# One activation buffer's low half, 64 bytes further on, in the token mixers as well

## The chip, the core and the metric

One Trainium2 chip; the kernel runs on one of its cores. The metric is the device time of one execution in microseconds, and of several executions the median. The profile is one execution of the same program recorded by the hardware profiler; its times count from the first instruction.

## What is computed

A decoder layer on 512 tokens of width 1024, in float32: a SwiGLU feed-forward network (width 2816), then a token mixer, then a second feed-forward network, each between a norm before and a norm after it.

```python
for l in range(DEPTH):
    x = x + 0.5 * rms_norm(swiglu_ffn(rms_norm(x, norm_pre[l, 0]), ffn1_w_in[l], ffn1_w_out[l]), norm_post[l, 0])
    mixed = token_mixer(rms_norm(x, norm_pre[l, 1]), w_mix_in[l], ...)
    x = x + rms_norm(mixed, norm_post[l, 1])
    x = x + 0.5 * rms_norm(swiglu_ffn(rms_norm(x, norm_pre[l, 2]), ffn2_w_in[l], ffn2_w_out[l]), norm_post[l, 2])
```

The mixer projects the normed x with one matrix (`h @ w_in`, 3592 columns), runs two recurrences over chunks of tokens (HGRN2 and mLSTM heads) and projects their outputs with `w_out`.

## The kernel before

**Two parts instead of one float32.** Every large product is made of three matmuls in the form float32r: each operand is split into a high part (a rounded copy, ScalarE) and a low part (what the rounding lost, VectorE), and high x high, high x low and low x high are summed in PSUM. So each buffer of activations or weights holds a high half of 1024 words per partition and a low half of 1024 words.

**Where the activations lie.** The transposed activations lie in four buffers `xq0` to `xq3`, made in `Layer.__init__` (L101 to L106). Each is one quarter: 256 tokens by half of the 1024 features. `xq0` has the first 256 tokens and features 0 to 511, `xq1` the same tokens and features 512 to 1023, `xq2` and `xq3` the other tokens. `xq0` alone is 32 words longer than the others (`2 * STEP`, `STEP` = 16 words = 64 bytes). There are two views of it. `self.xh[0]` is the view of the feed-forward networks: its low half begins 16 words later than the end of its high half. `self.xq[0]` is the view of the mixers: its low half follows at once, as in the other quarters. `xh` is used by `part` (L334, which writes it) and by `open_ffn` (L538, which makes the networks' operands of it); `xq` is used by `to_t` (L328, which writes it) and by `xop` (L153), through which every matmul of the mixers reads it.

**Where the weights lie.** One buffer `w` has four slots of 2048 words. `lie` (L207) puts a slot's contents at a displacement out of `LIES` (L64): 0, -16, -80 or 48 words, in another order for the mixers' wide weights ("mix": -16 first) than for the networks' first layers ("any": 0 first).

**What the mixers do with the quarters**, in order of time:

- `head4` (L508): four products `head_mm` (L498, its matmuls are L503), each 24 matmuls for the first 256 tokens: eight high x high, eight that read the activations' low half, eight that read the weights' low half. The weights are stationary, 256 columns of activations stream by.
- `forget_gates` (L1106): the same four products for the other 256 tokens, by `in_mm` and `in_k` (L489; matmuls L493): 24 matmuls each, of `xq2` and `xq3` alone.
- `job_f` (L937): eight products over all tokens, also by `in_k` (L493): for each of eight feature blocks six matmuls, and in the first four blocks one of the six reads the low half of `xq0`.
- `job_rows` (L1284, matmuls L1291): 32 matmuls for the gates' rows, four of them on the low half of `xq0`.
- `job_t` (L953), `mix_out0` and `mix_out1`: here the activations are stationary (128 x 128) and 512 columns of weights stream by, three matmuls at a time in `mm3` (L146; L148 high x high, L149 high x low, L150 low x high). L150 loads the activations' low half.

Between these stand small float32 matmuls and transposes of the recurrences. Which weights are loaded, split and freed when is planned by `weights` and `feed` ahead of use; the mixers fill the recurrences' waits with `job_*` work by `fill`.

The feed-forward networks' first layers are 7 products for each pair of column blocks (`prod`, matmuls L559). The product "p1" reads `xq0`: 24 matmuls in a row, of which the second eight read its low half, 64 bytes further on already. The second layers are L816 and L824.

Of the kernel before, what the change touches and what calls it, by code (L numbers as in the profile page):

```python
# [16 lines left out]
D = 1024  # L17
# [5 lines left out]
RAW, WBUF, PAD, LATE, NEXT, FRONT, STEP = 3, 4, 128, 112, 64, 96, 16  # L23
PAIRS = NF // 2
HALF = T // 2
KH = ND // 2
# [40 lines left out]
class Load:  # L67


    def __init__(self, key, src, a, b, ring="raw", depth=3, ahead=3, group=None):  # L70
        self.key, self.src, self.a, self.b, self.ring, self.depth, self.ahead = key, src, a, b, ring, depth, ahead
        self.group = group
# [12 lines left out]
class Layer:  # L85
    def __init__(self, ctx, tc, aps):
        self.tc, self.nc = tc, tc.nc
        self.__dict__.update(aps)
        nc = self.nc
        pool = lambda name, **kw: ctx.enter_context(tc.tile_pool(name=name, bufs=1, **kw))  # L90
        self.cp, self.wp, self.sp, self.psp = pool("cp"), pool("wp"), pool("sp"), pool("psp", space=PSUM)
        self.uid, self.hold = 0, ()
        self.wt, self.free, self.slot = None, deque(), {}

        self.ident = self.cp.tile([P, P], F32, name="ident")
        make_identity(nc, self.ident)
        self.nhalf = self.cp.tile([P, 8], F32, name="nhalf")
        nc.gpsimd.memset(self.nhalf, -0.5)
        self.xs = self.cp.tile([P, NT, D], F32, name="xs")

        xq = {n: self.cp.tile([P, 2 * D + 2 * STEP * (n == 0)], F32R, name=f"xq{n}") for n in (1, 2, 3, 0)}  # L101
        self.xt = [xq[n] for n in range(4)]
        self.xq = [t[:, : 2 * D].rearrange("p (b k t) -> p b k t", b=2, k=KH) for t in self.xt]

        x0 = self.xt[0].rearrange("p (b x) -> p b x", b=2)[:, :, :D].rearrange("p b (k t) -> p b k t", k=KH)
        self.xh = [x0, *self.xq[1:]]  # L106
        self.prm = self.cp.tile([P, 36], F32, name="prm")

    def nm(self, s):
# [42 lines left out]
    def xop(self, k, part, t0, t1):  # L152
        q = self.xq[2 * (t0 // HALF) + k // KH]  # L153
        return q[:, part, k % KH, t0 % HALF : (t1 - 1) % HALF + 1]
# [175 lines left out]
    def part(self, i, h, src):  # L330

        pv = self.turn(src, h)
        v = slice(i * P, (i + 1) * P)
        dst = self.xh[h][:, :, :, v]  # L334
        yield
        self.nc.scalar.copy(dst[:, 0], pv)
        yield
        self.nc.vector.tensor_tensor(dst[:, 1], pv, dst[:, 0].bitcast(F32), op=ALU.subtract)
        yield
        self.nc.scalar.copy(self.xf[h][:, :, v], pv)  # L340
        yield
# [189 lines left out]
    def open_ffn(self, ctx):  # L531

        hp = self.hpool = ctx.enter_context(self.tc.tile_pool(name=self.nm("hp"), bufs=1))
        self.hf = hp.tile([P, NF, T], F32, name=self.nm("hf"))
        self.xf = [self.hf[:, j : j + 2, :].rearrange("p a (b t) -> p (a b) t", t=HALF) for j in (NF - 4, NF - 2)]
        sq = [hp.tile([P, 2 * D + PAD], F32R, tag="s", bufs=3, name=self.nm("sq")) for _ in range(3)]
        self.sq = [self.both(self.place(t, LATE)) for t in sq]
        xq = [self.both(x) for x in self.xh]  # L538
        self.stay = [self.place(t, NEXT) for t in sq]
        self.left = {"p1": xq[0], "p2": xq[1], "p4": xq[3], "p5": xq[2], "p6": self.sq[2], "p7": self.sq[1], "p3": self.sq[0]}  # L540
        self.left.update({"c1": xq[0], "c2": xq[1], "c3": xq[0], "c4": xq[1]})
        self.left.update({"e1": xq[2], "e2": xq[3], "e3": xq[2], "e4": xq[3]})
        self.gs, self.held, self.copies = [], {}, []
        self.hs, self.bank, self.later, self.u, self.q, self.had = deque(), {}, deque(), {}, {}, set()
# [1171 lines left out]
```

## Time and profile before

| | us |
|---|---|
| median of 3 runs | 948.15 |
| the runs | 946.64, 948.79, 948.15 |
| the profiled execution, its time | 947.97 |
| the profiled execution, first to last instruction | 946.2 |
| TensorE (PE) busy | 937.4 |
| VectorE (DVE) busy | 776.1 |
| ScalarE (ACT) busy | 489.4 |
| GpSimd (POOL) busy | 121.2 |
| first matmul of the mixers (L503) to the last (L150) | 344.3 to 609.5 |

PE is the engine of the matmuls, PEld its weight loads, which run beside the matmuls. A group of instructions is shown as `line engine operation tile<-tiles`, its count, busy time and mean duration in ns. A matmul's recorded duration (276 ns and the like) is longer than the distance from one matmul to the next, since matmuls are pipelined: the distance is read from the chain of waits, where a row is the start in us, the length in us, and how many instructions of one line follow each other without a gap (16.32 us for 144 matmuls are 113.3 ns from one to the next).

### The profile page before, as it was taken

Reading aid. Unit: us, or ns where it says so; the run is one execution under the profiler, and the core shown is the slowest. Engines: PE = TensorE matmul, PEld = TensorE weight load, DVE = VectorE, ACT = ScalarE, POOL = GpSimd, SP = SyncE. Lnnn points to the kernel's source line nnn. Section 1 sums busy time; section 2 is a strip of 40 time slices with the busy share of each in tenths; the row PEclk is TensorE's granted clock in tenths of the full one; section 3 lists DMA queues with packets and bytes.
Section 4 is the critical chain, followed back from the end, with each engine's and each line's share of the span. In section 5 each row is a group of like instructions: output and inputs, shape, how many; then the busy total and the mean of one; then the engine's idle time right before and its main releaser. Section 6 shows DMA issues by size and latency. Waiting matters only on the chain.

```text
span 946.2 us, 18146 instructions
## 1 busy us (share of the span) xinstructions
PE 937.4 (99%) x7531; PEld 903.5 (95%) x7531; DVE 776.1 (82%) x1052; ACT 489.4 (52%) x691; POOL 121.2 (13%) x176
## 2 busy tenths in 40 slices
PE   9999999999999999999999999999999999999997
PEld 7999999999999999998887888899999999999997
DVE  6899999999789786698846665798998899988984
ACT  7645444555446457956632444664444444654541
POOL 3530000000001045200001310353000000000102
PEclk9999999999999999999999999999999999999999
DMA  9244343244232034321312124324333333124212
GB/s 319 84 134 134 106 141 111 91 131 119 97 108 85 23 92 126 98 67 46 89 45 68 45 89 139 107 68 135 112 112 118 107 112 112 67 90 135 70 44 89
DMA packets 81677, 96.13 MB, mean 102 GB/s; under 512 B 4117, under 2 KB 61497, under 8 KB 81594
## 3 DMA queue, kind: packets, MB, share of 16 engines
q1 hardware_dynamic: 81306, 94.44, 31.6%
q8 instruction: 59, 0.97, 0.4%
q10 hardware_dynamic: 288, 0.52, 0.2%
q14 instruction: 24, 0.20, 0.1%
HBM read 92.85 MB, written 2.10 MB: 100 GB/s over the span
## 4 chain that ended last, share of the span: by engine, by line
PE 62%; ACT 1%; DVE 0%; issue 0%; POOL 0%; DVEq 0%; POOLq 0%; ACTq 0%
PE ps L559 23%; PE ps L816 8%; PE ps L493 6%; PE ps L148 5%; PE ps L150 5%; PE ps L149 5%; PE ps L824 4%; PE ps L1206 2%; PE ps L316 1%; PE ps L503 1%; PE ps L1380 0%; PE ps L1291 0%; PE ps L1487 0%; PE ps L1460 0%; PE ps L1246 0%; PE ps L1484 0%
## 5 line engine op out<-in xcount | busy, mean ns | idle before, releaser
L242 ACT CAST w<-raw 128x1024 fp32r<-128x1024 f32 (+1 forms) x228 | 235.5, 1039 | 252.5 <-PE ps L559 89.7
L244 DVE TENSOR_TENSOR w<-raw,w 128x1024 fp32r<-128x1024 f32 (+1 forms) x228 | 283.2, 1248 | 42.6 <-ACT w L242 42.4
L559 PE MATMUL ps<-xq,w 128*128 128x256 f32 x2016 | 237.9, 277 | 0.0
L559 PEld LDWEIGHTS ps<-xq,w 128*128 128x128 f32 x2016 | 233.4, 188 | 0.0
L559 PE MATMUL ps<-sq,w 128*128 128x256 f32 x1440 | 169.8, 276 | 0.0
L559 PEld LDWEIGHTS ps<-sq,w 128*128 128x128 f32 x1440 | 166.2, 188 | 0.0
L816 PE MATMUL ps<-w,hs 128*128 128x256 f32 x1344 | 158.1, 276 | 0.3
L816 PEld LDWEIGHTS ps<-w,hs 128*128 128x128 f32 x1344 | 154.8, 188 | 0.7 <-DVE hs L752 0.7
L258 DVE TENSOR_TENSOR raw<-raw,raw 128x1024 f32<-128x1024 f32 x64 | 80.1, 1251 | 0.7
L148 PE MATMUL ps<-w,xq 128*128 128x512 f32 x192 | 78.9, 411 | 0.1
L150 PE MATMUL ps<-w,xq 128*128 128x512 f32 x192 | 74.9, 392 | 0.0
L149 PE MATMUL ps<-w,xq 128*128 128x512 f32 x192 | 74.9, 391 | 0.0
L404 POOL TENSOR_SCALAR col<-col 128x1 f32<-128x1 f32 x24 | 10.5, 438 | 494.4 <-ACT junk L403 494.3
L493 PE MATMUL ps<-xq,w 128*128 128x256 f32 x480 | 58.0, 282 | 0.0
L493 PEld LDWEIGHTS ps<-xq,w 128*128 128x128 f32 x480 | 56.8, 189 | 0.5 <-issue 0.5
L258 POOL TENSOR_TENSOR raw<-raw,raw 128x1024 f32<-128x1024 f32 x16 | 43.1, 2697 | 51.6 <-DVE w L244 42.3
L148 PEld LDWEIGHTS ps<-w,xq 128*128 128x128 f32 x192 | 36.1, 188 | 8.3 <-issue 0.9
L150 PEld LDWEIGHTS ps<-w,xq 128*128 128x128 f32 x192 | 36.0, 188 | 8.2 <-DVE xq L323 0.3
L149 PEld LDWEIGHTS ps<-w,xq 128*128 128x128 f32 x192 | 36.2, 188 | 6.7 <-issue 0.2
L751 ACT CAST hs<-hf 128x1024 fp32r<-128x1024 f32 x28 | 29.4, 1051 | 22.2 <-PE ps L824 22.2
L824 PE MATMUL ps<-w,hs 128*128 128x256 f32 x336 | 40.4, 276 | 0.0
L824 PEld LDWEIGHTS ps<-w,hs 128*128 128x128 f32 x336 | 39.1, 188 | 0.0
(250 smaller groups left out, 1143.1 us busy)
## 6 DMA issues: line engine op xcount, KB each, us to landing
raw<-in_ffn_w_in_dram SPq DMA_DIRECT2D x88, 512.0 KB, 3.8
raw<-in_ffn_w_out_dram SPq DMA_DIRECT2D x44, 512.0 KB, 3.7
raw<-in_w_mix_in_dram SPq DMA_DIRECT2D x28, 512.0 KB, 3.7
raw<-in_w_mix_out_dram SPq DMA_DIRECT2D x8, 512.0 KB, 3.7
out_dram<-xs SPq DMA_DIRECT2D x8, 256.0 KB, 2.1
xs<-in_x_dram SPq DMA_DIRECT2D x6, 256.0 KB, 6.3
gpost<-in_norm_post_dram SPq DMA_DIRECT2D x3, 512.0 KB, 4.7
gpre<-in_norm_pre_dram SPq DMA_DIRECT2D x2, 512.0 KB, 4.0
```

The costliest lines, as they stand in the source:

```text
L148: mm(ps, sh, mh, start=start, stop=False, **kw)
L149: mm(ps, sh, ml, start=False, stop=False, **kw)
L150: mm(ps, sl, mh, start=False, stop=stop, **kw)
L242: nc.scalar.copy(hi, raw)
L244: self.low = nc.vector.tensor_tensor(lo, raw, hi.bitcast(F32), op=ALU.subtract)
L258: (nc.vector if late else nc.gpsimd).tensor_tensor(o, o, c, op=ALU.add)
L493: mm(ps[:, u0:u1], w[:, a, k, :], self.xop(k, b, u0, u1), start=k + n + m == 0, stop=k == ND - 1 and n == 2, skip_group_check=True,)
L559: self.nc.tensor.matmul(ps[:, c], wb[b][:, k, v], left[d][:, k, :], start=first and a + n + k == 0, stop=n == 2 and k == KH - 1, skip_grou ...
L751: self.nc.scalar.copy(hi, src)
L816: mm(out, a[kk][:, i * P : (i + 1) * P], w[:, b, kk, QUARTER * v : QUARTER * (v + 1)], start=begin and c == kk == n == 0, stop=kk == 1 and ...
L824: mm(ps[:, QUARTER * c : QUARTER * (c + 1)], A[a][:, c], B[b], start=begin and c == n == 0, stop=n == 2, skip_group_check=True,)
L1206: nc.tensor.matmul(sc[:, 64 * m : 64 * m + 64], k8[:, m], q8[:, m], start=True, stop=True)
```

## The change

The two views become one: the low half of `xq0` lies 64 bytes further on for the mixers too. The buffer's length and place stay as they were.

```diff
-        self.xq = [t[:, : 2 * D].rearrange("p (b k t) -> p b k t", b=2, k=KH) for t in self.xt]
-
-        x0 = self.xt[0].rearrange("p (b x) -> p b x", b=2)[:, :, :D].rearrange("p b (k t) -> p b k t", k=KH)
-        self.xh = [x0, *self.xq[1:]]
+
+        parts = lambda t, x: t[:, : 2 * x].rearrange("p (b x) -> p b x", b=2)[:, :, :D].rearrange("p b (k t) -> p b k t", k=KH)
+        self.xq = [parts(t, D + STEP * (n == 0)) for n, t in enumerate(self.xt)]
...
-        dst = self.xh[h][:, :, :, v]
+        dst = self.xq[h][:, :, :, v]
...
-        xq = [self.both(x) for x in self.xh]
+        xq = [self.both(x) for x in self.xq]
```

No instruction, DMA or wait is added, removed or moved; on every engine the instructions stand in the same order with the same waits. What differs is the address of one operand in 16 matmuls of L503, 32 of L493, 4 of L1291 and 48 of L150 (as its stationary operand), and in the four VectorE instructions that write that half (L323).

## The prediction

> **What bounds the kernel now.** I read the page first: its engine totals, the clock, the chain that ended last and the matmul groups.
>
> ```profile
> span 946.2 us, 18146 instructions
> ...
> PE 937.4 (99%) x7531; PEld 903.5 (95%) x7531; DVE 776.1 (82%) x1052; ACT 489.4 (52%) x691; POOL 121.2 (13%) x176
> ...
> PEclk9999999999999999999999999999999999999999
> ...
> PE 62%; ACT 1%; DVE 0%; issue 0%; POOL 0%; DVEq 0%; POOLq 0%; ACTq 0%
> ```
>
> PE is busy for 99% of the span at full granted clock, and nothing but PE has more than 1% of the chain. Next come PE's waits between 333 and 640 us, which cover the mixers (columns: total us, times, longest).
>
> ```profile
> PE ps L503 <- ACT w L242: 0.3, 1, 0.3
> ```
>
> That is the only wait of a matmul on another engine that this window lists. So in the mixers a nanosecond that a matmul takes more or less is a nanosecond of the kernel's time, and no other engine stands ready to take a gain back. The change adds, removes and moves no instruction; all it can do is alter how long the matmuls are that read the moved half, or that follow them. So the third view is that of the instructions that touch the quarters (minimum, median and maximum duration in ns, then first and last start).
>
> ```profile
> L493 PE MATMUL ps<-xq,w x480: 276/281/681, 357.7 to 422.5; 128*128 128x256 f32 x160
> ...
> L824 PE MATMUL ps<-w,xq x252: 276/276/276, 237.5 to 912.1; 128*128 128x256 f32 x126
> ...
> L149 PE MATMUL ps<-w,xq x192: 387/389/402, 428.4 to 609.3; 128*128 128x512 f32 x192
> ...
> L503 PE MATMUL ps<-xq,w x96: 276/281/384, 344.3 to 357.6; 128*128 128x256 f32 x96
> ```
>
> The same shape, 256 columns, has a median of 276 ns in L824 and of 281 ns in L493 and L503. The matmuls have two paces. The chain of waits tells what they are worth, in rows of one line without a gap (start, us, what); the second fence is the same view over a later window.
>
> ```profile
> 351.33 2.83 PE ps L503 x24
> ...
> 355.04 2.83 PE ps L503 x24
> 357.87 33.92 PE ps L493 x288
> ...
> 396.49 10.60 PE ps L493 x90
> ...
> 409.48 4.10 PE ps L493 x36
> ...
> 415.30 4.30 PE ps L493 x36
> ...
> 421.33 1.43 PE ps L493 x12
> 422.77 3.76 PE ps L1291 x32
> ```
>
> ```profile
> 870.93 16.32 PE ps L816 x144
> ```
>
> 16.32 / 144 = 113.3 ns is the fast pace. 33.92 / 288 = 117.8 ns is the slow one, 4.4 ns more, and it lasts: it is there in L503, goes through all of 288 matmuls of L493, and is there again in the 90 behind it (117.8 ns), while 36 matmuls of the same line at 409.48 us, after some float32 matmuls, run fast (113.9 ns). So the pace is a state that a stretch keeps until something disturbs it, not a property of a line.
>
> **What 64 bytes do, by rows of the kernel before.** The networks' p1 product already reads the low half in its new place. Here is one p1 (24 matmuls of `xq0`, eight of them on the displaced half) and the product after it, which has no such half; then the two products after a slow stretch.
>
> ```profile
> 745.37 2.89 PE ps L559 x25
> ```
>
> ```profile
> 748.14 2.83 PE ps L559 x25
> ```
>
> ```profile
> L559 PE MATMUL ps<-xq,w 128*128 128x256 f32 x23 | 2.9, 281 | 0.0
> ```
>
> ```profile
> L559 PE MATMUL ps<-xq,sq 128*128 128x256 f32 x24 | 2.9, 276 | 0.0
> ```
>
> The first pair: 2.89 against 2.83 us, so a visit of eight matmuls to the displaced half costs about 0.06 us when the pace is fast. The second pair (the p1 from 622.75 to 625.3 us, then the product from 625.6 to 628.1): a p1 that is entered slow (281 ns) hands over a fast pace (276 ns). So the displaced half has both effects, a price and a reset, and the mixers get both.
>
> **The change part by part.** The sums are made against the profiled execution, 947.97 us (span 946.2 and 1.8 around it), 0.18 below the median 948.15.
>
> What there is to gain: the slow pace in the mixers. (24 + 24 + 288) x 4.4 ns = 1.49 us up to 391.8 us; the rows behind it against 113.3 ns give 0.40, 0.02, 0.22 and 0.07 = 0.71 us, and L1291 3.76 - 3.63 = 0.13 us. For the 512-column matmuls I take stretches from two places, 434.0 to 438.1 and 545.5 to 559.9 us:
>
> ```profile
> L150 PE MATMUL ps<-w,xq 128*128 128x512 f32 x6 | 2.4, 394 | 0.0
> L149 PE MATMUL ps<-w,xq 128*128 128x512 f32 x6 | 2.3, 391 | 0.0
> ```
>
> ```profile
> L149 PE MATMUL ps<-w,xq 128*128 128x512 f32 x22 | 8.6, 389 | 0.0
> L150 PE MATMUL ps<-w,xq 128*128 128x512 f32 x22 | 8.6, 389 | 0.0
> ```
>
> There too are two paces, 389 ns and 2 to 5 ns more. The averages over all of L149 and L150 stand on the page:
>
> ```profile
> L150 PE MATMUL ps<-w,xq 128*128 128x512 f32 x192 | 74.9, 392 | 0.0
> L149 PE MATMUL ps<-w,xq 128*128 128x512 f32 x192 | 74.9, 391 | 0.0
> ```
>
> They are 3 and 2 ns above 389, 0.96 us together; with 2 ns for L148, 0.38 us, it is 1.3 us. All slow pace in the mixers is thus 1.49 + 0.71 + 0.13 + 1.3 = 3.6 us, and no change of pace there can gain more.
>
> What there is to lose: visits. L503 makes 4 (four matmuls each), L493 32, L1291 4, and 48 weight loads are displaced in L150: 88 visits. A visit of one matmul is not in the trace; by the p1 row it costs between nothing and 0.06 us, so between 0 and 5.3 us in all.
>
> Now step by step.
>
> 1. L503: two of the four products run slow now (the two x24 rows, 117.9 ns); of the first two no row shows the whole, and I take them as fast. Two visits at a fast pace cost 2 x 0.06 = +0.12 us; the other two, at a slow pace, gain what is fast behind them, about eight matmuls each, -0.07 us. +0.05.
> 2. The next 96 matmuls of L493 (`in_mm`) read no `xq0`. If the last visit of L503 resets the pace they are fast: 96 x 4.4 = -0.43 us. A p1 has eight displaced matmuls in a row, L503 four, so I take half: -0.2.
> 3. The eight `job_f`, 384 matmuls of L493: in the first half of each the visits come every six matmuls. The p1 visit is eight matmuls long and its 60 ns are spread over the matmuls behind it as well, so I expect that six matmuls don't suffice to settle, and that this half runs slow: 24 x 4.4 = 0.11 us. The second half has nothing to disturb it and may settle fast: 0.04 us to settle. 8 x 0.15 = 1.2 us, against now 192 x 4.4 = 0.84 of the 288 and 0.72 of the rows behind, 1.56 us. -0.36 if it settles each time; if it never does, 384 x 4.4 = 1.7 us, +0.13. Middle: -0.1.
> 4. L1291: four visits, a stretch that is slow already; 0.
> 5. L148 to L150: 16 groups of three belong to a stretch that is slow now, some 32 to one that runs at 389 ns. A displaced load in every group of three there means the slow pace or a little above it: between 2 and 10 ns for each of 96 matmuls, 0.2 to 1 us, and some 0.03 us to settle behind each of six such stretches. +0.7.
> 6. The second network starts with whatever pace it is handed, and its first p1 products reset that as they do now; 0.
>
> Sum: 0.05 - 0.2 - 0.1 + 0.7 = +0.45 us: 947.97 + 0.45 = 948.4, and for a median, 0.18 higher, **948.6 us**. Nothing covers these edits, as PE waits for nobody; and no queue, VectorE's four writes among them, has other work than before.
>
> Two rules of the Trainium skill speak against any effect. "TensorE: Matmul & The Clock Gate", Part 2, says that PE reads the streaming operand and the weight load through two independent ports, so that loading the next weights takes nothing from the running matmul; "SBUF — State Buffer", "Who interferes with whom", says that PE and ACT never wait on anyone. By them the sum would be 0. The p1 row speaks against that, as two products with the same shapes differ by 0.06 us; it doesn't show which reads meet.
>
> **The rivals.**
>
> *No effect.* Visits of one matmul may be too short to matter at either pace, and the resets too weak. For it: the 32 and the 48 visits are of one matmul or load, where the p1 visit has eight. Against it: the pace is a state that lasts, so small pushes can have long tails. 947.97, or 948.15 as a median: 0.20.
>
> *The resets win (faster).* If four displaced matmuls, or one, always bring back the fast pace, the 1.49 and 0.71 us of L503 and L493 go but for 0.4 us of visits, and the 512-column matmuls lose half of their 1.3 us: -1.8 - 0.65 = -2.45 us, 945.7. For it: the p1 at 622.75 us. Against it: half of `job_f` has a visit every six matmuls. 0.10.
>
> *Each visit pays on its own (slower).* If a push of one matmul at a fast pace must be worked off in full, as after p1, each visit in a fast stretch costs up to 0.06 us and the stretches don't settle between visits. With 30 ns for each of 88 visits it is +2.6 us, 950.7. It decides from a price of about 22 ns a visit on (88 x 22 ns = 1.9 us), with nothing saved at the resets. For it: the p1 price. Against it: a slow stretch can't lose it a second time, and many visits lie in slow stretches. 0.16.
>
> **How the numbers follow.** The forecast, pushes and resets that nearly cancel, has 0.54, no effect 0.20, faster 0.10, slower 0.16. Forecast and no effect both lie within 0.2% of the median (1.9 us, about what a measurement of this kernel can tell from no change): 0.74 the same, 0.10 faster, 0.16 slower. The range reaches from 946.3 (three quarters of the resets' gain) to 950.5 (most of the visits' price); the bounds -3.6 and +5.3 us both need every unknown at its end.
>
> **What would show it.** Right: in L503 and the 96 matmuls behind it the mean falls from 281 towards 276 ns; the chain's row of 288 matmuls gets shorter than 33.92 us; L150 and its neighbours between 545.5 and 559.9 us rise above 389 ns. Wrong: L493 all at 281 ns as before and L149 and L150 at 389 (no effect); L493 at 276 throughout (the resets win); L493 or L148 to L150 above their slow paces of 281 and 394 ns (the visits pay). The prediction would fall as a whole if an engine other than PE waited or was waited for in the mixers.

## The result and the profile after

The changed kernel has a median of 949.29 us (17 runs, 948.72 to 950.49), the kernel before 947.26 us beside it (17 runs, 946.64 to 949.27). The ratio is 1.0018, 95% interval 1.0012 to 1.0025: slower, by about 1.7 us (the two medians lie 2.0 us apart), and within the 0.2% that the prediction called no change. Its forecast was +0.45 us.

In the changed kernel every line behind the diff has a number lower by one: L502 was L503, L492 was L493, L147 to L149 were L148 to L150. Its page, and then PE's waits between 333 and 640 us, where no row follows the head line:

```profile
span 947.2 us, 18146 instructions
...
PE 938.9 (99%) x7531; PEld 904.6 (96%) x7531; DVE 776.2 (82%) x1052; ACT 489.5 (52%) x691; POOL 120.3 (13%) x176
...
L147 PE MATMUL ps<-w,xq 128*128 128x512 f32 x192 | 79.0, 412 | 0.1
L149 PE MATMUL ps<-w,xq 128*128 128x512 f32 x192 | 75.1, 393 | 0.0
L148 PE MATMUL ps<-w,xq 128*128 128x512 f32 x192 | 75.0, 391 | 0.0
```

```profile
engine line waited for: us in total, times, longest us
```

PE is still the only bound, and it waits for nobody. The 512-column matmuls are up by 0.1 or 0.2 us a line against the page of before, where L148 stands so:

```profile
L148 PE MATMUL ps<-w,xq 128*128 128x512 f32 x192 | 78.9, 411 | 0.1
```

The chain of waits through the first mixer:

```profile
352.09 2.80 PE ps L502 x24
...
355.77 2.81 PE ps L502 x24
358.57 33.92 PE ps L492 x288
...
397.27 10.40 PE ps L492 x90
```

The two products of 24 took 2.83 us before and take 2.80 and 2.81; the 90 took 10.60 us and take 10.40. The long row of 288 is 33.92 us in both. These two profiled executions differ by 0.99 us (947.97 and 948.96), and the mixers hold little of that. I cut the trace into stages, from the start of each stage's first matmul to that of the next stage's:

| us | before | after |
|---|---|---|
| the first 200 matmuls | 29.02 | 29.71 |
| first network, first layers | 193.33 | 193.31 |
| first network, second layers | 120.42 | 120.52 |
| `head4` with its transposes | 13.38 | 13.32 |
| the 288 of L493/L492 | 33.92 | 33.92 |
| the rest of L493/L492, among float32 matmuls | 30.98 | 30.91 |
| `job_rows` | 5.46 | 5.48 |
| 512 columns, projections | 131.93 | 132.16 |
| 512 columns, output projection | 49.73 | 49.88 |
| second network | 330.04 | 330.03 |

0.69 us is at the very start, a stage that took between 29.0 and 30.1 us in the profiles of this study, whichever kernel it was. The mixers give +0.27 us. So this pair of executions does not show the 1.7 us, and the experiments had to find it.

### The profile page after: what moved, and what is told of

The parts are those of the page before. It is cut to its first block, busy times and chain, and to the rows that moved or that the text cites. A ratio compares the mean times of both kernels' runs of the same rounds, so it can differ in the third digit from the quotient of the medians.

```text
span 947.2 us, 18146 instructions
## 1 busy us (share of the span) xinstructions
PE 938.9 (99%) x7531; PEld 904.6 (96%) x7531; DVE 776.2 (82%) x1052; ACT 489.5 (52%) x691; POOL 120.3 (13%) x176
## 4 chain that ended last, share of the span: by engine, by line
PE 98%; DVE 1%; ACT 0%; issue 0%; POOL 0%; DVEq 0%; POOLq 0%; ACTq 0%
PE ps L558 45%; PE ps L815 17%; PE ps L823 7%; PE ps L492 6%; PE ps L147 5%; PE ps L149 5%; PE ps L148 5%; PE ps L1205 2%; PE ps L315 1%; PE ps L502 1%; PE ps L1379 0%; PE ps L1290 0%; PE ps L136 0%; PE ps L143 0%; PE ps L1486 0%; PE ps L1245 0%
## 5 line engine op out<-in xcount | busy, mean ns | idle before, releaser
L147 PE MATMUL ps<-w,xq 128*128 128x512 f32 x192 | 79.0, 412 | 0.1
L149 PE MATMUL ps<-w,xq 128*128 128x512 f32 x192 | 75.1, 393 | 0.0
L148 PE MATMUL ps<-w,xq 128*128 128x512 f32 x192 | 75.0, 391 | 0.0
L492 PE MATMUL ps<-xq,w 128*128 128x256 f32 x480 | 57.9, 282 | 0.0
L492 PEld LDWEIGHTS ps<-xq,w 128*128 128x128 f32 x480 | 56.7, 189 | 0.5 <-issue 0.5
L147 PEld LDWEIGHTS ps<-w,xq 128*128 128x128 f32 x192 | 36.1, 188 | 8.4 <-issue 0.9
L149 PEld LDWEIGHTS ps<-w,xq 128*128 128x128 f32 x192 | 36.0, 188 | 8.3 <-DVE xq L322 0.3
L148 PEld LDWEIGHTS ps<-w,xq 128*128 128x128 f32 x192 | 36.2, 188 | 6.8 <-issue 0.2
```

The lines of the kernel that those rows point to most:

```text
L147: mm(ps, sh, mh, start=start, stop=False, **kw)
L148: mm(ps, sh, ml, start=False, stop=False, **kw)
L149: mm(ps, sl, mh, start=False, stop=stop, **kw)
L492: mm(ps[:, u0:u1], w[:, a, k, :], self.xop(k, b, u0, u1), start=k + n + m == 0, stop=k == ND - 1 and n == 2, skip_group_check=True,)
```

## The experiments

**The theories.** *Visits:* each read of the displaced half costs something by itself, most likely in the 48 weight loads, where the pair of profiles shows it. *Pace:* the visits of L503 decide which of the two paces the long stretch behind them gets; since the profile of before had the slow one already, the loss then is in those of its runs that have the fast one. *No effect* is the third. The first four kernels displace the low half for one part of the mixers, or nowhere, and repeat the kernel before.

### Projections alone, output projection alone

In both kernels the mixers read through a view `xm`. The first has it displaced up to the recurrences' outputs and at its old place for the output projection, the second the other way round.

```diff
+        self.xm = self.xh
...
-        q = self.xq[2 * (t0 // HALF) + k // KH]
+        q = self.xm[2 * (t0 // HALF) + k // KH]
...
+                self.xm = self.xq
                 for i in range(NT):
                     self.to_t(i, self.y[:, i], (0,))
```

> The displaced half for the projections alone (L503, L493, L1291 and the 32 loads of the four job_t); the 16 loads of the output projection find it at the old place. Theory, that the price lies with displaced loads beside 512 streaming columns: two thirds of the loads are left, so L148 to L150 lose about 0.25 of the 0.4 us that the profile of the change shows there, none of it behind 560 us, and the time is 0.5 to 1.5 us above the kernel before. Rival, that single executions draw their paces by chance and the place has no part in it: the time is the same as that of the kernel before within 0.3 us.

> The displaced half for the output projection alone: 16 displaced loads, nothing else. Theory: L148 to L150 before 545 us run as in the kernel before, only the part behind it slows, by 0.1 to 0.2 us; the time is 0 to 0.6 us above the kernel before. Rival, chance: nothing tells the two parts apart, within 0.3 us of the kernel before.

Projections alone: 948.91 us (948.52 to 950.17, 11 runs) beside 947.45 for the kernel before, ratio 1.0015 (1.0006 to 1.0024). Output projection alone: 948.4 us (946.66 to 950.55, 11 runs), 1.001 (1.0001 to 1.0018). The second is the telling one: up to 560 us, where the output projection begins, it is the kernel before, address for address, and yet its chain through the first mixer reads

```profile
352.38 2.83 PE ps L504 x24
...
356.09 2.74 PE ps L504 x24
358.83 32.64 PE ps L494 x288
...
396.23 10.22 PE ps L494 x90
```

(L504 is L503 of before, L494 is L493). 32.64 / 288 = 113.3 ns: the undisplaced stretch can have the fast pace throughout. With the same addresses and the same work ahead of it, it had the slow pace in the profile of before, so these do not fix its pace. Below, the pace that an execution happens to get here is called its draw; the prediction took one draw for the kernel's nature. The output projection with 16 displaced loads took 49.92 us, against 49.70 to 49.74 in profiles without: so the loads cost something too.

### No displacement anywhere

```diff
-        self.xh = [x0, *self.xq[1:]]
+        self.xh = self.xq
```

> No displaced half at all, in the networks neither. Theory, that a p1 at a slow pace is handed on fast: without it the slow pace that follows the start of each network lasts, up to 1700 matmuls at 4.4 ns, so the time is 3 to 15 us above the kernel before and products of L559 stand at 281 ns by the dozen. Rival, that the displacement only costs 0.06 us at each p1: 1.1 us less than the kernel before.

958.37 us (957.31 to 959.11, 4 runs), ratio 1.0113 (1.0099 to 1.0127). Taking the displaced half away from the networks loses 11 us. The chains of waits from 600 and from 640 us, first of this kernel, then the stretch from 640 us of the changed one:

```profile
613.75 5.46 PE ps L559 x48
```

```profile
639.99 60.07 PE ps L559 x510
```

```profile
640.00 60.06 PE ps L558 x529
```

In the same 60 us it does 510 matmuls where the changed kernel does 529, 117.8 against 113.5 ns each: its second network drew the slow pace and, with nothing to reset it, kept it to the end (from its 300th matmul on 306.02 us, against 295.75 before). Its first network drew the fast one and took 192.83 us, 0.5 less than in the kernel before: that is what the p1 visits cost. The x48 row shows the price of one of them, 5.46 us against 5.51 us in the profile of before at the same place:

```profile
613.59 5.51 PE ps L559 x48
```

Here is what a displaced half does where it works: 0.05 us for each p1, and 10 us saved when the draw is bad.

### The kernel before, again

The code is that of the kernel before.

> The kernel before, once more, for a second profile of the same program. Theory: the slow stretch of 288 matmuls of L493 is there again at 117.8 ns, since the order and the addresses fix the pace. Rival, chance: the stretch has another pace in another execution, and the time of the two profiles differs by 1 us or more in the mixers. The ratio of times is 1 within 0.1%.

947.84 us (946.76 to 948.79, 10 runs), ratio 1.0003 (0.9994 to 1.0012): the kernel before agrees with itself within 0.1%. Its profiled execution took 948.21 us and had the 288 at 33.92 us again. The expected row came, but not for the expected reason: in the output projection's kernel the same order and addresses went with the fast pace.

### Streams and loads apart

Two kernels split the change by how the half is read. In the first, L503, L493 and L1291 read the high half of `xq0` in place of its displaced low half; the 48 displaced loads stay. In the second it is the other way round: L150 loads the high half, and the streams of L503, L493 and L1291 stay displaced.

```diff
+    def hop(self, k, part, t0, t1):
+        return self.xop(k, 0 if 2 * (t0 // HALF) + k // KH == 0 else part, t0, t1)
...
-                    ps[:, u0:u1], w[:, a, k, :], self.xop(k, b, u0, u1),
+                    ps[:, u0:u1], w[:, a, k, :], self.hop(k, b, u0, u1),
...
```

> The changed kernel, but L503, L493 and L1291 read the high half of xq0 where they read its displaced low half (at the place's old relation), so high x high is taken twice there and the result is not the layer's; the 48 displaced weight loads of L150 stay. Theory: they cost what the profiles show behind L148 to L150, 0.25 + 0.15 us, in each execution, and leave the stretch of 288 matmuls of L493 free to be slow (33.9 us) or fast (32.6 us) by chance as in the kernel before; median 0.3 to 0.8 us above the kernel before, fastest run under 947.8. Rival, that the loads are the whole price: 1.5 to 2 us above, no run under 948.2.

> The changed kernel, but L150 loads the high half of xq0 in place of its displaced low half (the result is not the layer's); the displaced reads of L503, L493 and L1291 stay. Theory: L148 to L150 take as long as in the kernel before (131.9 and 49.7 us from their first to their last), but the stretch of 288 is slow in every execution, since the last visits of L503 and those of job_f disturb a fast one: median 0.8 to 1.5 us above the kernel before, no run under 947.9. Rival, that the streams cost nothing: the two groups of runs of the kernel before, near 947.0 and 948.5, are both there.

Loads alone: 947.27 us (946.67 to 948.0, 11 runs) beside 946.87 for before, ratio 1.0005 (0.9996 to 1.0015), +0.40 us. Streams alone: 948.61 us (947.79 to 949.08, 11 runs), 1.0017 (1.0008 to 1.0025), +1.74 us. The changed kernel itself, once more in the same series:

> The changed kernel once more, for a second profile. Theory: 33.92 us for the 288 matmuls again, L148 to L150 within 0.05 us of the first profile, 1.5 to 2 us above the kernel before. Rival, chance: a fast stretch of 288 (32.6 us) in this profile.

949.13 us (948.29 to 949.82, 8 runs), 1.0023 (1.0013 to 1.0033), +2.26 us; 0.40 + 1.74 = 2.14 us, so the two parts add up, as far as their intervals tell. That of the loads alone reaches below 1, so their +0.40 us rests on the lengths of stages in the profiles (below). Most of the loss is in the streams, in 52 matmuls. The chains, of loads alone, of streams alone, and of the changed kernel:

```profile
355.21 2.74 PE ps L505 x24
357.95 32.64 PE ps L495 x288
...
395.35 10.22 PE ps L495 x90
```

```profile
355.43 2.81 PE ps L505 x24
358.23 33.92 PE ps L495 x288
...
396.93 10.40 PE ps L495 x90
```

```profile
355.89 2.81 PE ps L502 x24
358.70 33.92 PE ps L492 x288
...
397.40 10.40 PE ps L492 x90
```

(L505 and L495 are L503 and L493.) The kernels with displaced streams have 33.92 us, and so it is in all four profiles of such kernels (the two of the changed kernel, projections alone, streams alone). Of the profiles with undisplaced streams some have 32.64 and some 33.92. Four profiles alone could be chance. The runs of this series say the same: of the 31 of the kernel before 28 took 947.25 us or less and the slowest 947.90, while the 19 with displaced streams start at 947.79 us, and only four of them lie below 948.30. The pace is not drawn any more: it is set to slow.

How it is set is seen in the changed kernel's trace, in groups by line over narrow windows: behind the first matmuls of the third product of L502, at its end, and the same for the fourth product.

```profile
L502 PE MATMUL ps<-xq,w 128*128 128x256 f32 x8 | 1.1, 281 | 0.0
```

```profile
L502 PE MATMUL ps<-xq,w 128*128 128x256 f32 x7 | 1.0, 276 | 0.0
```

```profile
L502 PE MATMUL ps<-xq,w 128*128 128x256 f32 x6 | 0.8, 277 | 0.0
```

```profile
L502 PE MATMUL ps<-xq,w 128*128 128x256 f32 x5 | 0.8, 281 | 0.0
```

The third product begins slow (281 ns) and ends fast (276), the fourth begins fast and ends slow. Between beginning and end of each lie its four displaced matmuls. Worked out from the starts of the matmuls, the distances across them are 117, 118 | 122, 116, 119, 119 | 118, 114, 124, 118, 113, 114 ns in the third product and 113, 114 | 119, 112, 117, 118 | 119, 119, 117, 118 ns in the fourth, the displaced four between the bars. **Four displaced matmuls in a row turn the pace over, whichever it is.** The five profiles with displaced streams (those above and the one of the four matmuls below) hold 19 such visits; in 16 the other pace stands behind them, and the other three come while the pace is slow and are followed by a pause before it has settled. The last product of `head4` thereby hands on a slow pace to the 288.

### The slow pace made by other means

If the loss is the handed-on pace, then it must come without any displaced activations in the mixers as well. This is the kernel before; only the weights of the last product of `head4` lie 64 bytes earlier.

```diff
-        at = LIES[kind]
+        at = LIES["mix" if self.items_key == ("mix", 3) else kind]
...
+        self.items_key = it.key
```

> The kernel before, with the fourth projection's weights 64 bytes earlier, so that 24 matmuls of L503 and 24 of L493 run at the relation that the displaced p1 has, ahead of job_f. Theory: behind them the 192 matmuls of job_f start fast whatever came before: L493 from its first to the next float32 matmul takes under 33.4 us, and the time is 0.2 to 0.8 us under the kernel before. Rival, that only a p1's own order resets: 33.9 us as before, and no gain.

948.86 us (948.18 to 949.16, 11 runs) beside 946.87, ratio 1.0018 (1.001 to 1.0027): the whole loss of the changed kernel but for its loads. The chain:

```profile
355.83 2.87 PE ps L504 x24
358.70 33.98 PE ps L494 x288
```

The 24 matmuls with the moved weights are slow themselves (2.87 us, 120 ns each) and hand on the slow pace. It was meant to try whether moving the weights resets the pace as moving the activations does in p1; it doesn't. Neither the theory nor its rival had this loss: the moved weights leave the slow pace behind them. This also bears on what the kernel before draws: to force one stretch slow can only cost 2.0 us if most of its runs have it fast.

### Four matmuls

The last test takes from the changed kernel only the last visit of L502: the fourth product's four displaced matmuls read the high half of `xq0`. All 32 visits of L492, those of L1290 and all 48 loads stay.

```diff
-                    ps[:, :HALF], w[:, a, k, :], self.xop(k, b, 0, HALF), ...
+                    ps[:, :HALF], w[:, a, k, :], self.xop(k, b if len(self.head) < 3 or k >= KH else 0, 0, HALF), ...
```

> The changed kernel, but the fourth product of L503 reads the high half of xq0 in its four displaced matmuls (the result is not the layer's): four matmuls of 7324 lie elsewhere. Theory, that a visit of four turns the pace over, slow to fast and fast to slow: the third product's visit makes it fast, the fourth's, now gone, made it slow ahead of in_mm and job_f. So the 96 matmuls of in_mm are fast in every execution (10.9 us), job_f pays 27 ns for each of 16 single visits, and L493 takes 33.07 us for its 288 in place of 33.92; the time is 0.7 to 1.1 us under the changed kernel, 0.8 to 1.3 above the kernel before. Rival, that the visits of job_f themselves make the stretch slow: 33.5 us or more and within 0.3 us of the changed kernel.

The chain, and the 95 matmuls of L492 between 359 and 369.5 us, here and then in the changed kernel:

```profile
352.37 2.81 PE ps L502 x24
...
356.05 2.74 PE ps L502 x24
358.79 33.07 PE ps L492 x288
...
396.63 10.40 PE ps L492 x90
```

```profile
L492 PE MATMUL ps<-xq,w 128*128 128x256 f32 x95 | 10.9, 276 | 0.0
```

```profile
L492 PE MATMUL ps<-xq,w 128*128 128x256 f32 x92 | 11.0, 281 | 0.0
```

The row of 288 falls from 33.92 to 33.07 us for four matmuls out of 7531. The 96 of `in_mm` all run at 113.3 ns. The 192 of `job_f` behind them, with 16 single visits, hold the rest: 33.07 - 288 x 113.3 ns = 0.43 us, 27 ns a visit. At the slow pace the same 16 visits cost nothing: 33.92 us with them and without.

The time does not agree. 948.97 us (948.12 to 949.36, 11 runs) beside 947.82 for before (14 runs): +1.15 us, ratio 1.001 (1.0001 to 1.0019). Against the changed kernel, which was measured in other series, on other chips (949.29 and 949.13), that is 0.2 to 0.3 us less by the medians, where the row has 0.85 and the theory had 0.7 to 1.1: by the time alone its rival, within 0.3 us, would do as well. The profiled execution took 948.32 us, the two of the changed kernel 948.96 and 949.11. But it was the second fastest of the eleven runs. The faster eight of the 14 runs of before have a median of 947.3 us; with 0.43 us for the visits of `job_f` and the 0.24 and 0.42 us of the table below, about 948.4 us was due. So the row shows what the fourth product's visit does where it is left out, and not that most executions of this kernel have this row. Without its last visit the fourth product keeps the pace that it starts with. It starts fast in all five profiles whose third product is turned to fast ahead of it; in the seven in which these two products read nothing from a moved place the third product ends slow, and the fourth starts fast in three and slow in four.

### An attempt at a faster version

If it is the distance between weights and activations that counts, moving the low half of a network's weights 448 bytes further might reset the pace as the displaced activations do, and without them the mixers would be undisturbed. That 448 bytes one way stand for 64 the other way is an assumption, which no run here tests by itself. The first kernel does this in p1 for two of its weights, with no displaced activations anywhere; the second also for one of the mixers' weights.

```diff
+FAR = {("p1", 2), ("p1", 3)}
...
-        self.xh = [x0, *self.xq[1:]]
+        self.xh = self.xq
...
+            if it.far:
+                w = tuple(self.wt[:, o + m : o + m + D].rearrange("p (k t) -> p k t", k=a) for m in (0, D + 112))
```

> No displaced half of the activations anywhere; in its place the low half of the weights of p1 for the third and fourth pair of column blocks lies 448 bytes further, which is 64 bytes less within 512, the relation that the displaced half had: 16 matmuls a network in place of some 90. Theory, that a run of eight matmuls at that relation and then the common one sets the fast pace whoever moves: each network is reset early and pays about 0.05 us twice in place of about nine times, 0.5 to 0.9 us less than the kernel before. Rival, that the reset needs the activations' side or every p1: a slow second network as with no displaced half, 5 us or more above the kernel before.

> As z1, and in the mixers the third projection's low half of weights lies 448 bytes further and in_mm takes its eight feature blocks one part after the other, as p1 does, so that a run of eight stands ahead of the last 24 matmuls of in_mm and of job_f. Theory: those 24 + 192 matmuls of L493 are fast in every execution (24.5 us for 216), runs of the group that is slow there now gain 0.9 us or more beside the gain of z1, the others nothing. Rival, that the fast stretch is chance and no run of eight sets it: 25.4 us for 216 and the time of z1.

969.78 us (4 runs) and 969.84 us (5 runs) beside 948.6, ratio 1.0225 (1.0211 to 1.0239) for both: the worst of all. The chain of the first from 640 us:

```profile
639.89 60.21 PE ps L564 x511
```

117.8 ns a matmul, as in the second network with no displacement. Here the first network is slow too: its first layers take 200.13 us against 193.3. By the starts of the matmuls the pace is 113.3 ns up to the first eight moved ones, 120 ns across them and 117.8 ns from there on. The moved weights stand at the end of their product, they throw the pace into the slow one, and nothing brings it back. In the second of the two kernels the eight moved matmuls of `in_mm` do the same, 113.3 ns ahead of them, 120 across them, 117.8 behind, and the 216 matmuls took 25.44 us, as the rival had it. No distance by itself tells what resets. A third profile of the kernel before went along:

> The kernel before for a third profile. Theory: most of its runs on the second chip stood between 946.3 and 947.3 us, 1.3 to 1.5 us under the two profiled executions, and that is the stretch of 288 matmuls of L493 at the fast pace, 32.64 us in place of 33.92, with 0.2 us behind it. Rival: it is 33.92 us again, and the spread of its runs comes from the loads at the start.

948.3 us (947.04 to 949.58, 10 runs), ratio 1.0 (0.9991 to 1.0009); the 288 took 33.92 us once more. No kernel of this study beats the kernel before.

### What adds up

Lengths of stages from the profiles, by how the 288 were entered:

| us | streams undisplaced, drew slow | undisplaced, drew fast | displaced |
|---|---|---|---|
| 288 matmuls | 33.92 | 32.64 | 33.92 |
| the rest of L493 | 30.98 | 30.67 | 30.91 |
| profiles | before (three) and no displacement | output alone, loads alone, first of the attempts | changed (two), projections alone, streams alone |

The 512-column stages don't depend on that: 131.86 to 131.93 us (projections) and 49.70 to 49.74 us (output) without displaced loads, 132.13 to 132.16 and 49.88 to 49.92 us with them, but for one output stage of 49.55. That is 0.25 + 0.17 = 0.42 us for 48 loads, 9 ns each. A run of before with the fast draw loses 1.28 + 0.24 + 0.42 = 1.94 us by the change, one with the slow draw 0.35 us. The medians differ by 2.0 us, the means by 1.8.

In some series the runs of before stand in two groups: in that of the four matmuls eight between 946.63 and 947.95 and six between 948.72 and 949.54 us, in the first series ten up to 947.34, one at 947.87 and six from 948.15 on. In others they do not: the 27 beside the first four kernels lie between 946.64 and 949.66 without a gap in the middle, and the 31 beside the split into streams and loads have no upper group at all. So how often the slow pace is drawn differs from series to series, and these were run on different chips. The changed kernel has no run below 948.29 us. All three profiled executions of before happened to draw slow, so that its fast draw was seen only in kernels that are the same up to that place, or nearly so; that the lower group is the fast draw is inferred from the lengths of the stages. And the sum does not close: ten fast draws and six slow ones would lose 1.3 us on average by the table, where the means of the first series differ by 1.8. The other 0.5 us is not explained.

## Why the prediction was right or wrong

The range, the sign and "within 0.2%" were right, and so was the frame: nothing but the pace of matmuls moved. The sum was a quarter of what came. That the time came nearer, 948.6 against 949.29 us, is luck: the base of the sum, 947.97 us, was an execution with the slow draw, 0.7 us above the median 947.26 of 17 runs, and made up for part of the loss that the sum lacked. Of the signs that it named, only the last came: L148 to L150 rose above 389 ns, while the 96 matmuls stayed at 281 ns and the row of 288 at 33.92 us.

- *What bounds the kernel:* right. No wait came or went.
- *What there is to gain* was the premise that failed first. The chain of before was read as the kernel's nature. Its time lay only 0.18 us below the median of three runs, but two of these three were of the upper group themselves, and the profile drew the slow pace together with the shortest start of all profiles (29.02 us), which hid it. By their times most runs have no slow 288 to gain from; they have it to lose, 1.28 + 0.24 us.
- *Step 1* (L503, +0.05): -0.06 us in the pair; too small to tell from the draws, 13.24 to 13.40 us over all profiles.
- *Step 2* (96 of `in_mm`, -0.2) is the step that failed. "If the last visit of L503 resets the pace" carried the eight matmuls of a p1 over to four. Eight hand on the fast pace, from fast and from slow; four turn it over, and the last turn ends slow. Against the profiled execution that is 0, where -0.2 stood. Against a run with the fast draw it is +0.43 us, and since the slow pace goes on through the 192 matmuls of `job_f`, 1.28 us in all, the greater part of the loss. The four-matmul experiment shows it in the row of 288 of one profile.
- *Step 3* (`job_f`, -0.1): nothing to be seen, as the stretch is slow anyway; beside float32 matmuls -0.07 us. The price of a single visit, 27 ns at the fast pace (in the one profile that has such visits), is near the 30 ns of the rival in which each visit pays; the rival's 88 such visits aren't there, since most fall into slow stretches, as was held against it.
- *Step 4* (L1291, 0): +0.02 us.
- *Step 5* (512 columns, +0.7): right in kind, too large: +0.42 us. Between 546.1 and 560.5 us, the place that was to show it, the changed kernel's groups by line read

```profile
L147 PE MATMUL ps<-w,xq 128*128 128x512 f32 x22 | 8.6, 393 | 0.0
L148 PE MATMUL ps<-w,xq 128*128 128x512 f32 x22 | 8.6, 390 | 0.0
L149 PE MATMUL ps<-w,xq 128*128 128x512 f32 x21 | 8.2, 390 | 0.0
```

  where 389 ns stood: above it, as was said, but by 1 and 4 ns, and most on the matmul behind the displaced load.
- *Step 6* (second network, 0): right in the pair. Twice, in output alone and streams alone, its later part took 0.7 us more (296.44 against 295.74): another draw, which is not the change's.
- *No effect* falls, and with it the sum of 0 that the prediction drew from two rules of the Trainium skill ("TensorE: Matmul & The Clock Gate", Part 2; "SBUF — State Buffer", "Who interferes with whom"). Where the operands lie moves this kernel by 1.1% (no displacement) and 2.2% (the first of the attempts), with the same instructions. Whether either rule is itself wrong is not shown: which reads meet is open, and PE waited for no other engine in the mixers of the changed kernel.

What stays open: which reads meet in the slow pace, why four matmuls turn it and eight reset it, what decides the draw after a break such as the transposes between the third and the fourth product, and why the kernel without the last visit took longer than its row allows. And the runs of one kernel also spread within a group by up to 1.5 us, of which the start (29.0 to 30.1 us for the first 200 matmuls) is the largest part that the profiles show.

## What to carry to other kernels

A profile is one draw: before a row is taken as what a kernel does, compare its time with the spread of the runs, and where they stand in two groups, ask which group the profile is from. Where a pace lasts until something disturbs it, a disturbance is priced by the state that it hands on to what follows, at the end of its stretch, and not by its own few nanoseconds. And a helpful displacement in one loop (24 matmuls, eight of them displaced in a row) is not carried over to a loop that reads the same buffer in fours and ones without measuring it there.

## What the hardware showed that was not expected

- Two paces of a 256-column float32r matmul, 113.3 and 117.8 ns, each kept over hundreds of matmuls: the slow one over 1776 matmuls of one line in 209.17 us in the kernel with no displacement.
- Reads of one displaced operand: eight in a row end fast whatever the pace was and cost 0.05 us; four in a row turn it over (16 visits of 16 behind which the pace could settle); a single one costs 27 ns at the fast pace, in one profile, and nothing at the slow one; a displaced weight load beside 512-column matmuls costs 9 ns.
- Moving the other operand works the other way: 24 matmuls with weights 64 bytes earlier took 120 ns each and left the slow pace behind them, and so did eight with the weights' low half 448 bytes further.
